# All 72 products of the conditioning row with the ada weights on VectorE

## The chip, the core and the metric

One core of one Trainium2 chip runs the whole layer as one program. The metric is device time in microseconds for one execution; three executions of the kernel before gave 561.93, 562.78 and 564.66 us, and their median, 562.78 us, is the number to beat or to miss. A profiled execution of the same program gives the rows that are shown below.

## What is computed

The reference is one decoder layer on 256 rows of 1024 columns: a half-step SwiGLU FFN (FFN 1), a mixer (attention beside an mLSTM), a second half-step FFN (FFN 2) and a last norm. Each of the three parts is modulated by a shift, a scale and a gate, which come from one row `c`:

```python
mod = (c @ w_ada[l] + b_ada[l]).reshape(B, N_MOD, D_MODEL)      # 9 vectors of 1024
sh1, sc1, g1, sh2, sc2, g2, sh3, sc3, g3 = [mod[:, None, i] for i in range(N_MOD)]
h = modulate(rmsnorm(x, ffn1_norm[l]), sh1, sc1)
x = x + 0.5 * (1 + g1) * swiglu(h, ffn1_w_gate[l], ffn1_w_up[l], ffn1_w_down[l])
h = modulate(rmsnorm(x, mix_norm[l]), sh2, sc2)
x = x + (1 + g2) * hybrid_mixer(h, ...)
h = modulate(rmsnorm(x, ffn2_norm[l]), sh3, sc3)
x = x + 0.5 * (1 + g3) * swiglu(h, ffn2_w_gate[l], ffn2_w_up[l], ffn2_w_down[l])
return rmsnorm(x, final_norm)
```

The product `c @ w_ada` has 9216 columns, which is 72 tiles of 128. These 72 tiles are what the change is about.

## The kernel before

**Layout.** Activations are held transposed: 128 columns on the partitions, 256 rows along the free dimension, eight such tiles `x_sb[:, d]`. Weights are the stationary side of TensorE's products. To keep precision, every weight chunk and every activation is split into a part of 12 bits and its rest, and each product is three matmuls (`mm3`): high by high, low by high, high by low.

**The weight stream.** `chunks` lists the weights in the order of their use, 1 MB each as a rule. `weights()` gives the next one: loads run three chunks ahead, splits one chunk ahead. A split of 1024 columns is two instructions: ScalarE copies the raw weights to `whi` (the 12-bit part), then VectorE subtracts and writes `wlo`. There are four raw buffers, five of `whi` and five of `wlo`; TensorE's products free the split ones.

**The ada tiles.** `ada(col, on_pool)` (L247) loads one tile of 128 x 1024 float32 (512 KB, three buffers named `ada`) and forms the sum of its product with `c_bc`, the row `c` on every partition. It has two ways to do so. With `on_pool` GpSimd multiplies (`prod`, one buffer) and ScalarE sums by copying it with an accumulator (`junk2`, shown as `junk<-prod`). Without, VectorE multiplies and sums in one fused instruction (`junk<-ada,c_bc`), followed by a short read of its accumulator.

**Who calls it.** In FFN 1 `adas(d)` (L402) asks for two tiles for each `d` from 1 on: the shift's one on GpSimd, the scale's one on VectorE; the two of `d` = 0 are asked for in the same way in the start. `fins(d)` then finishes them on VectorE (`fin`, `gs`, `sh`) and makes the modulated norm (`ht`, `hh`, `hl`), which TensorE needs as its moving operand. The other tiles are jobs in a list that `side(...)` (L543) pops at fixed places of FFN 1, the mixer and FFN 2; an argument 1 means GpSimd, 0 VectorE. Of the 72 tiles 43 go to GpSimd and ScalarE and 29 to VectorE; the last eight, during FFN 2, are all on VectorE.

**Order.** The start is written out in order (`ordered(True)`) up to the end of the step `d` = 0 of FFN 1. From there on a scheduler orders each engine's instructions by a simulation of their times, and each engine runs its own list strictly in that order. All loads are issued by the SP queue in program order throughout, so that an ada load that waits for a free buffer holds back the weight loads behind it.

**Stages of the profile.** The start lasts until the first real matmul at 17 us. FFN 1's gate and up products run until about 152 us, its down products until 222 us; then come the mixer, FFN 2, whose last product starts at 547 us, and the last norm. All instructions that go through the ordering helper carry the line L54, so the rows are told apart by tile names.

Of the kernel before, what the change touches and what calls it, by code (L numbers as in the profile page):

```python
# [43 lines left out]
class Ordered:  # L44
    """An engine whose instructions keep the order they are written in while on."""

# [14 lines left out]
def layer(ctx: ExitStack, tc: tile.TileContext, i, out: bass.AP):  # L61
# [39 lines left out]

# [1 line left out]
    c_row = wp.tile([1, D], F32, tag="ada", name="c_row", bufs=3)  # L103
# [6 lines left out]

    # c on every partition, the squares of x; the tensor engine's clock rises with use
    ones_m = const([P, P], F32, "ones_m")
# [47 lines left out]
    for h in range(NH):  # L160
        pool.memset(ohc[:, h, h:h + 1], 1.0)
    # rows h and 32 + h of block h: ones
    oh32 = const([36, NH, P], F32, "oh32")
# [6 lines left out]

# [1 line left out]
    SP = 1024  # L172
# [14 lines left out]
    def load_to(n):  # L187
        """Loads up to chunk n."""
        while len(raws) <= min(n, len(chunks) - 1):
            src = chunks[len(raws)]  # L190
            n1 = src.shape[-1]
            raw = raw_tile()[:, 0:n1]
            cuts = 1 if len(raws) > 3 else 2
            for k in range(cuts):
                sl = slice(k * n1 // cuts, (k + 1) * n1 // cuts)
                dma(raw[:, sl], src[:, sl])
            raws.append(raw)

    def split_piece():
        """Splits the next piece into a part of 12 bits and its rest."""  # L200
        if not parts or len(parts[-1]) * SP >= raws[len(parts) - 1].shape[-1]:
            parts.append([])
        raw, w = raws[len(parts) - 1], parts[-1]
        b = len(w) * SP
        m = min(SP, raw.shape[-1] - b)
        hi = wp.tile([P, SP], F32R, tag="whi", name=nm("whi"), bufs=5)
        lo = wp.tile([P, SP], F32R, tag="wlo", name=nm("wlo"), bufs=5)
        src = raw[:, b:b + m]
        act.activation(hi[:, 0:m], src, AF.Copy)
        dve.tensor_tensor(lo[:, 0:m], src, as32(hi[:, 0:m]), ALU.subtract)  # L210
        w.append((hi, lo))

    def split_to(n):
        """Splits up to chunk n."""
        n = min(n, len(chunks) - 1)
        while len(parts) <= n or len(parts[n]) * SP < raws[n].shape[-1]:
            split_piece()

    def weights(ahead=3):
        """The next chunk, split; loads run ahead by three chunks, splits by one."""  # L220
        n = used[0]
        used[0] += 1
        load_to(n + ahead)
        split_to(n + 1)
        return parts[n]
# [11 lines left out]

# [1 line left out]
    mod = const([P, 72], F32, "mod")  # L239
# [7 lines left out]
    def ada(col, on_pool=False):  # L247
        """mod[:, col] = (c @ w_ada) of the 128 columns from 128 * col."""
        t = wp.tile([P, D], F32, tag="ada", name=nm("ada"), bufs=3)
        dma(t, i["ada"][col])  # L250
        if on_pool:
            pr = wp.tile([P, D], F32, tag="prod", name=nm("prod"), bufs=1)
            pool.tensor_tensor(pr, t, c_bc, ALU.mult)
            junk = wp.tile([P, D], BF16, tag="junk2", name=nm("junk"), bufs=1)
            act.activation(junk, pr, AF.Copy, accum_out=mod[:, col:col + 1])
        else:
            junk = wp.tile([P, D], BF16, tag="junk", name=nm("junk"), bufs=1)
            dve.scalar_tensor_tensor(junk, t, 1.0, c_bc, ALU.mult, ALU.mult,
                                     accum_out=mod[:, col:col + 1])

# [30 lines left out]

# [1 line left out]
    def newton(r0, v, shape, tag, eps=EPS):  # L293
# [5 lines left out]
    def rstd_of(parts, ones=None, tag="m", pre=True, mid=None):  # L299
        """1/sqrt(mean over the partitions of the sum of parts + eps), on every partition."""  # L300
        ps = bank(tag)[:, 0:T]
# [16 lines left out]
    def norm_h(k, d, r, mid=None):  # L318
        """The modulated norm, split."""
        t = t256("ht", bufs=3)  # L320
        dve.scalar_tensor_tensor(t, x_sb[:, d], gs[k][:, d:d + 1], r, ALU.mult, ALU.mult)
        if mid:
            mid()
        act.activation(hh[:, d, 0:T], t, AF.Identity, bias=sh[k][:, d:d + 1])
        dve.scalar_tensor_tensor(hl[:, d, 0:T], t, sh[k][:, d:d + 1], as32(hh[:, d, 0:T]), ALU.add, ALU.subtract)

    def pre_h(k, d):
        """x * gain * (1 + scale), split: the norm before its row factor and shift."""
        act.activation(hh[:, d, 0:T], x_sb[:, d], AF.Copy, scale=gs[k][:, d:d + 1])
# [3 lines left out]
    def pre_shift(k):  # L333
        """The shift, split, as columns T and T + 1."""
        for c in range(2):
# [9 lines left out]
    def add_sq(d, eng):  # L345
        """Squares of x_d into acc; those of the last one stay apart."""
        s = t256("sq", bufs=3)
# [22 lines left out]

# [1 line left out]
    def finish(gh, gl, ft, g, u):  # L372
# [21 lines left out]
    def ffn(k, nxt):  # L394
        nfa = 3
        with tc.tile_pool(name=f"g{k}", bufs=1) as gp:
            gh = gp.tile([P, NF, T], F32R, name=f"gh{k}")
            gl = gp.tile([P, NF, T], F32R, name=f"gl{k}")
            if k == 0:
# [11 lines left out]
                def first(w, ps):  # L411
                    """Columns 0, the parts apart."""
                    for f4 in (0, 4):
# [7 lines left out]
                def outer(w, ps, d, stop, done=None):  # L421
                    """Columns d of 8 tiles of gates and ups."""
                    for ft in range(8):
# [6 lines left out]
                def inner(w, f2, pb, d0, stop):  # L430
                    """Columns d0 to d0 + 3 of one tile of gates and ups."""
                    for d in range(4):
# [110 lines left out]
    def side(*on):  # L543
        """Jobs on the side, on the pool engine (1) or not."""
        for o in on:
            if jobs:
                jobs.pop(0)(o)

# [1 line left out]
    jobs += scale_jobs(1) + gate_jobs(0) + shift_jobs(1) + gate_jobs(1) + scale_jobs(2) + shift_jobs(2)  # L550
    ffn(0, 1)

# [1 line left out]
    # x_m from the norm before its row factor  # L554
    px = [bank("a") for _ in range(4)]
# [11 lines left out]

# [1 line left out]
    with tc.tile_pool(name="fin", bufs=1) as fp:  # L569
# [10 lines left out]
def mixer(tc, nc, i, mp, L):  # L580
# [12 lines left out]
    def tiles(*done):  # L593
        """Two tiles of 128 columns of the input projection, transposed, before row factor and shift."""
        w = weights()
# [7 lines left out]
    def shifted(dst):  # L603
        """Applies row factor and shift."""
        def done(pb):
# [9 lines left out]

# [1 line left out]
    wTv = L["raw_tile"]()  # L617
# [10 lines left out]
    def fold():  # L628
        """Gate weights and query times key weights, taken through the headwise projections."""
        pg = bank("a")  # L630
# [12 lines left out]
        act.activation(wfold[:, 320:832], pqk, AF.Copy, scale=float(P) ** -0.5)  # L643
        # value weights less their mean over the head's channels: the group norm's centring
        vmean = mt([P, NH], "vmean")
# [4 lines left out]

# [1 line left out]
    xm = mt([P, NH, T + 3], "xm", tag="A")  # L652
# [39 lines left out]
    def spread(src):  # L692
        """src's rows, split, for a product that puts one of them on every partition."""
        act.activation(rows[0:4], src, AF.Copy)
# [6 lines left out]
    def gates():  # L701
# [11 lines left out]
        dve.tensor_scalar(gf, pgt[32:36, 0:T], bf, 0.0, ALU.add, ALU.min)  # L713
        # log1p(e) = ln(u) + (e - (u - 1)), u = fl(1 + e)
        lg = mt([NH, T], "lg", tag="R4")
# [12 lines left out]
        spread(nM)  # L728
        # eps * exp(-2 m), kept where its root and the root's square are finite
        em = st["em"] = mt([NH, T], "em", tag="R1")  # L730
# [53 lines left out]
    def m_factors():  # L784
        """The denominators and the group norm's row factor."""
        # 1 / (n sqrt(var / n^2 + eps)) = 1 / sqrt(var + eps n^2), n = max(|den|, exp(-m))
        prow, em = st["prow"], st["em"]
# [10 lines left out]

    # the first tile of the mix on its own: the others take the norm's place after its last use
    mix0 = [mt([P, T], name, F32R) for name in ("mix0h", "mix0l")]  # L800
# [10 lines left out]
    def m_out_pre(h):  # L811
        # (c * norm) * silu(z), (skip * x_conv) * silu(z)
        dve.scalar_tensor_tensor(cn[:, h], cn[:, h], sm[:, C_MN + h:C_MN + h + 1], zs[:, h], ALU.mult, ALU.mult)
        pool.tensor_tensor(xc[:, h], xc[:, h], zs[:, h], ALU.mult)
# [12 lines left out]

# [1 line left out]
    sc = 64 ** -0.5  # L829
# [47 lines left out]
    def turn(j):  # L877
        """Transposes the weights of two heads."""
        for e in range(2):
# [29 lines left out]

# [1 line left out]
    side(1, 0)  # L911
# [96 lines left out]
def _pack(a):  # L1008
    """Layout of the inputs for the kernel: transposes, tiles, zero padding."""
    f = np.float32  # L1010
# [80 lines left out]
```

## Time and profile before

| what | us |
|---|---|
| median of three executions | 562.78 |
| span of the profiled execution (first to last instruction) | 558.7 |
| median less span: what lies around the instructions | 4.1 |
| TensorE (PE) busy, mean granted clock 0.976 | 525.9 |
| VectorE (DVE) busy | 449.8 |
| ScalarE (ACT) busy | 323.9 |
| GpSimd (POOL) busy | 166.9 |

The profiled execution's own time is its span and the 4.1 us around it, which puts it at the median. Busy times of different engines overlap; an engine's idle time costs something only where TensorE waits for it in the end.

### The profile page before, as it was taken

How to read it: one execution, taken by the hardware profiler on the slowest of the kernel's cores; microseconds unless marked ns; L12 is line 12 of the kernel's file. 1: busy time of each engine (PE TensorE's matmuls, PEld its weight loads, DVE VectorE, ACT ScalarE, POOL GpSimd, SP SyncE). 2: the span in 40 equal slices, each digit the busy share in tenths (PEclk: the TensorE clock that was granted, in tenths of full speed). 3: DMA queues.
4: the chain of work that ended last, by engine and by line, in shares of the span. 5: the costliest groups of instructions: out<-in, count | busy, mean ns of one | idle time of the engine just before them, and what ended most of it. 6: DMA issues, size and time to landing. Idle time of an engine off the chain costs nothing.

```text
span 558.7 us, 10327 instructions
## 1 busy us (share of the span) xinstructions
PE 525.9 (94%) x4172; PEld 508.1 (91%) x4172; DVE 449.8 (81%) x626; ACT 323.9 (58%) x572; POOL 166.9 (30%) x107
## 2 busy tenths in 40 slices
PE   7799998999979999699989998999999999999992
PEld 7799998998979999698778888999999999999992
DVE  7989998999889989989987379789987767644423
ACT  5556556676665566567687665676545555544410
POOL 6313413346546766364431002400000000013321
PEclk9799999899989999899999999999999999999997
DMA  8998796367787879865743213478874555545002
GB/s 297 321 363 332 307 351 258 150 225 272 290 307 289 349 284 355 279 261 199 302 187 99 111 59 114 151 264 307 299 249 163 189 189 164 213 157 208 15 0 75
DMA packets 23952, 125.75 MB, mean 225 GB/s; under 512 B 2657, under 2 KB 2913, under 8 KB 14434
## 3 DMA queue, kind: packets, MB, share of 16 engines
q1 hardware_dynamic: 23906, 125.11, 60.8%
q8 instruction: 32, 0.52, 0.4%
q14 instruction: 14, 0.11, 0.1%
HBM read 124.05 MB, written 1.05 MB: 224 GB/s over the span
## 4 chain that ended last, share of the span: by engine, by line
PE 60%; DVE 18%; issue 11%; POOL 5%; ACT 5%; DMA 1%; SPq 0%; DVEq 0%; POOLq 0%; ACTq 0%
PE psa L54 29%; PE psb L54 16%; PE psm L54 14%; DVE wlo L54 8%; POOL prod L54 5%; DVE junk L54 3%; ACT whi L54 2%; ACT junk L54 1%; DVE gm L54 1%; DMA ada<-in_ada 1%; DVE ht L54 1%; DVE mx L54 1%; DVE wfold L54 1%; DVE x L54 1%; DVE hl L54 0%
## 5 line engine op out<-in xcount | busy, mean ns | idle before, releaser
L54 DVE TENSOR_TENSOR wlo<-raw,whi 128x1024 fp32r<-128x1024 f32 (+1 forms) x162 | 229.4, 1423 | 49.2 <-ACT whi L54 48.0
L54 ACT ACTIVATE whi<-raw 128x1024 fp32r<-128x1024 f32 (+1 forms) x162 | 167.6, 1043 | 74.9 <-PE psa L54 39.7
L54 POOL TENSOR_TENSOR prod<-ada,c_bc 128x1024 f32<-128x1024 f32 x43 | 115.2, 2678 | 129.7 <-ACT junk L54 87.0
L54 PE MATMUL psa<-hh,whi 128*128 128x258 f32 (+1 forms) x396 | 110.9, 286 | 4.2 <-DVE x L54 4.0
L54 PE MATMUL psa<-hh,wlo 128*128 128x258 f32 (+1 forms) x396 | 111.2, 286 | 1.3 <-DVE wlo L54 1.3
L54 PE MATMUL psa<-hl,whi 128*128 128x258 f32 (+1 forms) x396 | 110.5, 287 | 0.0
L54 PE MATMUL psb<-hh,whi 128*128 128x258 f32 (+1 forms) x320 | 93.0, 292 | 6.5 <-ACT hh L54 3.9
L54 PE MATMUL psb<-hh,wlo 128*128 128x258 f32 (+1 forms) x320 | 91.7, 288 | 0.0
L54 PE MATMUL psb<-hl,whi 128*128 128x258 f32 (+1 forms) x320 | 90.5, 286 | 0.0
L54 PEld LDWEIGHTS psa<-hh,whi 128*128 128x128 f32 x396 | 75.1, 192 | 4.7 <-DVE x L54 4.2
L54 PEld LDWEIGHTS psa<-hh,wlo 128*128 128x128 f32 x396 | 75.1, 191 | 1.5 <-DVE wlo L54 1.5
L54 PEld LDWEIGHTS psa<-hl,whi 128*128 128x128 f32 x396 | 75.0, 193 | 0.1
L54 PEld LDWEIGHTS psb<-hh,whi 128*128 128x128 f32 x320 | 61.6, 193 | 9.4 <-ACT hh L54 4.1
L54 PEld LDWEIGHTS psb<-hh,wlo 128*128 128x128 f32 x320 | 61.2, 192 | 1.0 <-issue 0.4
L54 PEld LDWEIGHTS psb<-hl,whi 128*128 128x128 f32 x320 | 61.2, 193 | 0.0
L54 POOL TENSOR_SCALAR u_out<-x,sm 128x256 f32<-128x256 f32 x8 | 8.3, 1041 | 166.3 <-DVE x L54 166.3
L54 PE MATMUL psm<-hh,wlo 128*128 128x256 f32 (+1 forms) x204 | 57.6, 285 | 0.1
L54 PE MATMUL psm<-hh,whi 128*128 128x256 f32 (+1 forms) x204 | 57.7, 285 | 0.0
L54 PE MATMUL psm<-hl,whi 128*128 128x256 f32 (+1 forms) x204 | 57.2, 284 | 0.0
L54 PE MATMUL psa<-gh,wlo 128*128 128x256 f32 x176 | 49.5, 282 | 0.0
L54 PE MATMUL psa<-gh,whi 128*128 128x256 f32 x176 | 49.5, 281 | 0.0
L54 PE MATMUL psa<-gl,whi 128*128 128x256 f32 x176 | 49.4, 281 | 0.0
(238 smaller groups left out, 1066.0 us busy)
## 6 DMA issues: line engine op xcount, KB each, us to landing
ada<-in_ada SPq DMA_DIRECT2D x72, 512.0 KB, 5.2
raw<-in_dn SPq DMA_DIRECT2D x22, 1024.0 KB, 5.4
raw<-in_guB SPq DMA_DIRECT2D x19, 1024.0 KB, 4.7
raw<-in_gu SPq DMA_DIRECT2D x18, 1024.0 KB, 7.3
raw<-in_gu SPq DMA_DIRECT2D x8, 512.0 KB, 7.8
raw<-in_wqk SPq DMA_DIRECT2D x4, 1024.0 KB, 7.5
raw<-in_wout SPq DMA_DIRECT2D x4, 1024.0 KB, 4.6
raw<-in_guA SPq DMA_DIRECT2D x4, 768.0 KB, 4.3
```

Source lines behind the costliest of these rows:

```text
L54: r = f(*a, **k)
```

## The change

`ada` loses its branch. The argument `on_pool` stays in the signature and is ignored, so that all callers, and the order of the jobs, stay as they are; every tile takes the fused instruction on VectorE. The buffers `prod` (but for its early use as `zeros`) and `junk2` are no longer used. Elsewhere the diff only takes out comments and docstrings.

```diff
     def ada(col, on_pool=False):
         t = wp.tile([P, D], F32, tag="ada", name=nm("ada"), bufs=3)
         dma(t, i["ada"][col])
-        if on_pool:
-            pr = wp.tile([P, D], F32, tag="prod", name=nm("prod"), bufs=1)
-            pool.tensor_tensor(pr, t, c_bc, ALU.mult)
-            junk = wp.tile([P, D], BF16, tag="junk2", name=nm("junk"), bufs=1)
-            act.activation(junk, pr, AF.Copy, accum_out=mod[:, col:col + 1])
-        else:
-            junk = wp.tile([P, D], BF16, tag="junk", name=nm("junk"), bufs=1)
-            dve.scalar_tensor_tensor(junk, t, 1.0, c_bc, ALU.mult, ALU.mult,
-                                     accum_out=mod[:, col:col + 1])
+        junk = wp.tile([P, D], BF16, tag="junk", name=nm("junk"), bufs=1)
+        dve.scalar_tensor_tensor(junk, t, 1.0, c_bc, ALU.mult, ALU.mult,
+                                 accum_out=mod[:, col:col + 1])
```

## Rows read from the trace of the kernel before

**Rows 1.** Stretches: length, busy us (instructions) by engine, granted clock, DMA share, GB/s

```profile
20.00:80.00 60.00, 59.97 (x490) 59.76 (x490) 57.24 (x75) 34.65 (x46) 19.01 (x7) 0.98 0.89 341
80.00:150.00 70.00, 66.31 (x536) 65.53 (x536) 64.82 (x75) 46.18 (x83) 29.84 (x11) 0.98 0.64 238
150.00:240.00 90.00, 81.94 (x640) 80.32 (x639) 81.90 (x72) 56.66 (x88) 51.98 (x27) 0.94 0.84 312
240.00:300.00 60.00, 57.01 (x433) 50.06 (x432) 56.83 (x106) 43.18 (x102) 23.65 (x12) 1.00 0.59 221
```

**Rows 2.** Waits of PE from 20 to 300 us: total us, times, longest

```profile
PE psa L54 <- DVE x L54: 4.0, 1, 4.0
PE psb L54 <- ACT gh L54: 2.8, 1, 2.8
PE psb L54 <- DVE half L54: 2.1, 1, 2.1
```

**Rows 3.** Instructions on prod, whole span: ns min/median/max, first and last start

```profile
L54 POOL TENSOR_TENSOR prod<-ada,c_bc x43: 2339/2512/4700, 8.7 to 282.5; 128x1024 f32<-128x1024 f32 x43
L54 ACT ACTIVATE junk<-prod x43: 1037/1046/1060, 11.1 to 287.2; 128x1024 bf16<-128x1024 f32 x43
```

**Rows 4.** The same view, 80 to 300 us alone

```profile
L54 POOL TENSOR_TENSOR prod<-ada,c_bc x34: 2369/2516/4700, 87.5 to 282.5; 128x1024 f32<-128x1024 f32 x34
```

**Rows 5.** Timeline at 155 us: start, us, engine, operation

```profile
155.04 2.40 POOL L54 TENSOR_TENSOR prod<-ada,c_bc 128x1024 f32<-128x1024 f32 x1 [1.26 <-ACT junk L54]
155.11 3.41 DVE L54 TENSOR_TENSOR wlo<-raw,whi 128x1024 fp32r<-128x1024 f32 x1
```

**Rows 6.** DVE groups by form, 0 to 300 us: busy us, mean ns, idle before

```profile
L54 DVE TENSOR_TENSOR wlo<-raw,whi 128x1024 fp32r<-128x1024 f32 x85 | 137.0, 1622 | 10.9 <-ACT whi L54 10.8
L54 DVE SCALAR_TENSOR_TENSOR junk<-ada,c_bc 128x1024 bf16<-128x1024 f32 x21 | 37.6, 1789 | 1.1 <-DMA ada<-in_ada 1.1
L54 DVE TENSOR_TENSOR gl<-gm,gh 128x256 fp32r<-128x256 f32 x22 | 18.6, 858 | 1.4 <-ACT gh L54 1.3
...
L54 DVE TENSOR_TENSOR fin<-mod,b 128x1 f32<-128x1 f32 x8 | 7.7, 968 | 0.1
...
L54 DVE TENSOR_TENSOR gm<-sl,half 128x256 f32<-128x256 f32 x8 | 6.5, 807 | 0.1
...
L54 DVE TENSOR_TENSOR sh<-mod,sm 128x1 f32<-128x1 f32 x8 | 3.4, 419 | 0.0
...
L54 DVE TENSOR_TENSOR gs<-fin,sm 128x8 f32<-128x8 f32 x2 | 2.5, 1240 | 0.0
L54 DVE TENSOR_TENSOR gm<-sl,psa 128x256 f32<-128x256 f32 x6 | 2.5, 410 | 0.0
```

**Rows 7.** The same view of DVE, 380 to 560 us

```profile
L54 DVE TENSOR_TENSOR wlo<-raw,whi 128x1024 fp32r<-128x1024 f32 x55 | 67.3, 1223 | 32.3 <-ACT whi L54 31.4
L54 DVE TENSOR_TENSOR gl<-gm,gh 128x256 fp32r<-128x256 f32 x22 | 9.2, 418 | 0.0
L54 DVE SCALAR_TENSOR_TENSOR junk<-ada,c_bc 128x1024 bf16<-128x1024 f32 x7 | 8.5, 1218 | 0.1
```

**Rows 8.** Timeline of the start, 8 to 18 us

```profile
8.63 0.18 DVE L54 TENSOR_SCALAR b<-sm 128x72 f32<-128x72 f32 x1
8.73 2.35 POOL L54 TENSOR_TENSOR prod<-ada,c_bc 128x1024 f32<-128x1024 f32 x1 [1.87 <-DVE ohr L54]
...
9.90 2.27 DVE L54 SCALAR_TENSOR_TENSOR junk<-ada,c_bc 128x1024 bf16<-128x1024 f32 x1 [1.08 <-DMA ada<-in_ada]
...
12.21 0.16 DVE L54 TENSOR_TENSOR fin<-mod,b 128x1 f32<-128x1 f32 x1
...
13.73 2.31 DVE L54 TENSOR_TENSOR sh<-mod,sm 128x1 f32<-128x1 f32 x1
...
17.03 0.80 PE L54 MATMUL psb<-hh,whi 128*128 128x256 f32 x2 [3.89 <-ACT hh L54]
```

**Rows 9.** Waits of POOL, whole span: total us, times, longest

```profile
POOL prod L54 <- DMA ada<-in_ada: 37.5, 5, 16.9
```

## The prediction, made before the changed kernel ran

> **What bounds the kernel now.** I read the busy times first: TensorE has work for 525.9 of 558.7 us, VectorE for 449.8. A mean over the span says little, because GpSimd's products all lie before 290 us, so I cut the span into stretches [rows 1]. The reader should see two things there. From 20 to 80 us TensorE has no gap. From 80 to 300 us it is idle for 3.7 + 8.1 + 3.0 = 14.7 us, and its granted clock is below 1 in two of the three stretches: 0.98 over 70 us and 0.94 over 90 us, which is worth 1.4 + 5.4 = 6.8 us of full-clock work. In all of these stretches VectorE is busy for over nine tenths of the time (57.2 of 60, 64.8 of 70, 81.9 of 90, 56.8 of 60 us), so it is the engine that runs late. The view of waits says the same [rows 2]: the longest waits of TensorE from 20 to 300 us end with VectorE (the residual `x`, `half`), or with ScalarE's `gh`, which itself follows VectorE's `gm`.
>
> Why VectorE is late is seen in the timeline and in its groups. At 155 us GpSimd starts a product of 2.40 us, and 0.07 us later VectorE starts a split that takes 3.41 us [rows 5]. The same split takes 1.223 us on the mean of 55 where no product runs [rows 7]. So VectorE's two-input work stands still while a product of GpSimd is under way. The groups up to 300 us, beside the same operations when undisturbed, give the total [rows 6, 7, 8]:
>
> - `wlo`: 137.0 - 85 x 1.223 = 33.0 us
> - `junk` on VectorE: 37.6 - 21 x 1.218 = 12.0 us
> - `gl`: 18.6 - 22 x 0.418 = 9.4 us
> - `fin`, `sh` and the wide `gs`, at 0.16 us each when undisturbed: 6.4 + 2.1 + 2.2 = 10.7 us
> - `gm<-sl,half`: 6.5 - 8 x 0.41 = 3.2 us (0.41 is the mean of its sister that reads PSUM)
>
> Together 68.3 us, or 1.59 us of VectorE's time for each of the 43 products.
>
> **The change part by part.** It removes 43 products of GpSimd, 2.51 us each, and 43 sums of ScalarE, 1.05 us each [rows 3]. It adds 43 fused instructions to VectorE; the price is that of the seven during FFN 2, where GpSimd multiplies nothing: 1.218 us [rows 7]. That adds 43 x 1.22 = 52.5 us and takes away about 68.3 us of standing still. Each tile moved is thus worth 1.59 - 1.22 = 0.37 us of VectorE's time.
>
> *From 80 to 300 us* lie 34 of the 43 [rows 4]: 34 x 0.37 = 12.6 us less for VectorE, in stretches where TensorE is idle for 14.7 us because of it. I count this in full. The bounds: GpSimd keeps other work (additions into `acc`, masks, the convolution's first tap), so not all of the 68.3 us need be the products'. If a fifth of it stays, a tile is worth 1.27 - 1.22 = 0.05 us, and the term 1.7 us. TensorE can't gain more than its idle 14.7 us.
>
> At this place a rule speaks of more. The Trainium skill (SBUF — State Buffer, Who interferes with whom) says that GpSimd and a VectorE instruction with two SBUF inputs share one read port as an exclusive lock, and that the second to issue waits out the whole instruction of the first. The rows agree in kind: 3.41 - 1.22 = 2.19 us of standing still beside a product of 2.40 us. If every product cost VectorE its full 2.51 us, a moved tile would be worth 1.29 us, VectorE would be relieved by 44 us, and the term would be capped by the 14.7 us; the sum would be 20.1 and the time 542.7 us. The groups show 1.59 us, since a product can also fall where VectorE reads PSUM or is itself first; I stay with the rows.
>
> *The clock.* After a long gap TensorE runs on at the lower of its two levels for a while; the stretch with the waits of 4.0 and 2.8 us is the one with 0.94 [rows 1, 2]. Those two gaps should shrink, not all vanish. I take half of the 6.8 us, 3.4, with bounds 0 and 6.8.
>
> *The start* runs in the written order. VectorE's first fused instruction took 2.27 us and the tiny `sh` 2.31 us, beside products of GpSimd [rows 8]. Undisturbed they cost 1.22 and 0.16 us, so 1.05 + 2.15 = 3.2 us go. The added fused instruction for the shift's first tile fits between the end of `b` at 8.81 us and the landing that starts the next one at 9.90; it ends at 10.03 and costs 0.13. So the first real matmul, now at 17.03 us, could come 3.0 us earlier. From 20 to 80 us the DMA share is 0.89 with TensorE never idle, and the loads behind the start move up less: the second weight chunk waits for an ada buffer that the first product frees at about 11.1 us and that is now free at 10.0. So 1.0 to 3.0 us; I take 2.0.
>
> *From 20 to 80 us* VectorE is relieved too, by 7 tiles' worth, but TensorE has no gap to close there: nothing. The cover is the load stream, and if it tears, see the second rival.
>
> *ScalarE* loses 45 us of sums and *GpSimd* about 108 us. Neither ends a wait of TensorE by its own load: nothing, beyond that `whi` and `gh` come a little sooner. *The SP queue*: an ada buffer is now freed by VectorE's instruction. Weight loads stand behind ada loads, but no split waits for a raw weight now (VectorE's `wlo` waits for `whi` alone, 10.8 us in 300 [rows 6]). I take nothing. *FFN 2* has all its eight tiles on VectorE already: nothing. After 300 us nothing changes.
>
> Sum: 12.6 + 3.4 + 2.0 = 18.0 us. Against the span of 558.7 that is 540.7; with the 4.1 us around it, 544.8 us, where the profiled execution and the median stand at 562.8. The bounds give 562.8 - (1.7 + 0 + 1.0) = 560.1 and 562.8 - (14.7 + 6.8 + 3.0) = 538.3.
>
> **The rivals.** *The gaps are of the order, not of the load.* TensorE's gaps stand at the ends of stages (the last `gh` before the down products, the last residual before the mixer). If they are the length of a chain and VectorE's place in its list, rather than its backlog, they stay, and only the lower bounds come: 559 to 560 us. For it: the two longest waits are single events at such ends. Against it: the chains through them run over splits and fused instructions that took 3.41 instead of 1.22 us.
>
> *VectorE stands before a load* (slower). GpSimd waited 37.5 us in five waits for ada tiles, 16.9 in the longest [rows 9], with only the next product behind it. On VectorE, which keeps its list's order, all splits, residuals and norms stand behind such an instruction, and TensorE waits for the splits. If the scheduler's idea of the landing is as early as it was for GpSimd, and all of it reaches TensorE, the price is 37.5 us against the gain of 18.0: about 582 us. It decides once more than 18 us of such waits come through. Against it: the 21 fused instructions that VectorE already runs up to 300 us wait for the same stream, and lost 1.1 us to it [rows 6].
>
> *The standing still is not the products' doing.* Then VectorE simply gets 41 x 1.22 = 50.0 us more from 20 to 300 us, where it has 260.8 of 280 busy: 310.8, which is 30.8 us too many, and the time is 562.8 + 30.8, about 594 us. Against it: the undisturbed 1.223 us over 55 splits, in a stretch without products. The Trainium skill has a rule on this side (Perfetto Trace Analysis, Optimizing Scalar/DVE Operations): if VectorE is saturated, handing some of its work to ScalarE or even GpSimd may make sense. The page adds that between VectorE and GpSimd it might not help, because of the port, as in [rows 5].
>
> **How the numbers follow.** The forecast's own range is 538 to 552 us, chance 0.62. A gain beyond it, below 538: 0.04 (the clock at the start may come up sooner too). The first rival, or a mixture of it with the forecast, 552 to 562 us: 0.20, of which 0.12 is faster than by 0.5% (below 560.0) and 0.08 within it. The second rival: 0.08 slower, and 0.02 where it just eats the gain. The third: 0.04. That makes 0.78 faster, 0.10 the same within 0.5%, which is about what a measurement of this kernel can tell from no change, and 0.12 slower. The range is 535 to 562 us: it takes in both ends of the bounds and the first rival, and leaves out the slower cases and a part of the unchanged ones.
>
> **What would show it.** Right: splits and `gl` up to 300 us at 1.22 and 0.42 us but for those beside GpSimd's `acc`; VectorE's busy time down by some 16 us although it has 43 instructions more; the first real matmul at 14 to 16 us; the waits for `x` and `gh` at the ends of FFN 1's parts shorter; the clock from 150 to 240 us nearer 1; nothing changed after 300 us but the offset. Wrong: fused instructions idle before ada loads, with the splits behind them late (second rival); gaps of the same length at the same places while VectorE has idle time (first); splits still at 1.6 us on the mean (third).

## The result, and the profile after

The changed kernel takes 547.66 us (median of four executions, 544.78 to 550.38) against 563.6 for the kernel before, measured beside it; the ratio is 0.9716 with a 95% interval of 0.9672 to 0.9759. The forecast was 544.8 us, with its own range from 538 to 552. The profiled execution has a span of 543.0 us, 15.7 less than before.

First the page of the changed kernel: busy time of each engine.

```profile
PE 520.8 (96%) x4172; PEld 502.2 (92%) x4172; DVE 419.6 (77%) x712; ACT 281.6 (52%) x486; POOL 48.8 (9%) x64
```

VectorE has 86 instructions more (43 fused ones and their reads of the accumulator) and is busy for 30.2 us less (449.8 before). The groups of VectorE up to 300 us show where that comes from; they answer to [rows 6] (busy us, mean ns, idle before).

```profile
L54 DVE TENSOR_TENSOR wlo<-raw,whi 128x1024 fp32r<-128x1024 f32 x89 | 108.7, 1227 | 15.4 <-ACT whi L54 15.3
L54 DVE SCALAR_TENSOR_TENSOR junk<-ada,c_bc 128x1024 bf16<-128x1024 f32 x64 | 77.9, 1218 | 8.0 <-DMA ada<-in_ada 7.8
L54 DVE TENSOR_TENSOR gl<-gm,gh 128x256 fp32r<-128x256 f32 x22 | 8.7, 417 | 0.0
...
L54 DVE SCALAR_TENSOR_TENSOR gm<-xm,sm,gm 128x256 f32<-128x256 f32 x12 | 5.6, 477 | 0.3 <-POOL gm L54 0.3
...
L54 DVE TENSOR_TENSOR gm<-sl,half 128x256 f32<-128x256 f32 x8 | 3.3, 416 | 0.0
```

The split fell from 1.622 to 1.227 us, `gl` from 0.858 to 0.417, `gm<-sl,half` from 0.807 to 0.416: the first two are now at the price they had before in stretches without products [rows 7], the last at that of its sister that reads PSUM [rows 6].

The stretches answer to [rows 1], with the start and the time after 300 us beside them (length, busy us of PE, PEld, DVE, ACT, POOL, granted clock, DMA share, GB/s).

```profile
0.00:20.00 20.00, 16.77 (x112) 15.76 (x112) 17.08 (x35) 8.36 (x12) 5.96 (x20) 1.00 0.86 319
20.00:80.00 60.00, 56.50 (x464) 55.87 (x465) 52.46 (x86) 29.22 (x35) 0.00 (x0) 1.00 0.90 351
80.00:150.00 70.00, 68.27 (x569) 67.87 (x568) 65.53 (x110) 39.52 (x68) 0.00 (x0) 1.00 0.83 311
150.00:240.00 90.00, 90.00 (x753) 88.52 (x751) 77.60 (x123) 46.53 (x72) 10.57 (x13) 1.00 0.81 297
240.00:300.00 60.00, 60.00 (x418) 49.25 (x418) 45.62 (x109) 39.01 (x103) 2.48 (x3) 1.00 0.48 175
300.00:380.00 80.00, 76.30 (x592) 72.69 (x591) 62.05 (x110) 48.32 (x93) 11.70 (x12) 0.98 0.48 171
```

The same two stretches of the kernel before, which [rows 1] does not have:

```profile
0.00:20.00 20.00, 13.96 (x78) 13.13 (x79) 16.19 (x25) 9.96 (x14) 10.65 (x22) 0.90 0.86 303
300.00:380.00 80.00, 77.99 (x602) 71.43 (x602) 58.25 (x108) 54.05 (x118) 13.64 (x13) 1.00 0.39 138
```

From 80 to 300 us TensorE is now idle for 1.7 us where it was for 14.7, and its granted clock is 1.00 where it was 0.94 to 1.00. But two stretches are worse than before: it is idle for 3.5 us from 20 to 80 us, where it had no gap, and for 3.7 us from 300 to 380 us (2.0 before).

The start answers to [rows 8]; the last three rows are TensorE's products that begin the first, the second and the third weight chunk.

```profile
8.78 1.21 DVE L54 SCALAR_TENSOR_TENSOR junk<-ada,c_bc 128x1024 bf16<-128x1024 f32 x1
...
10.03 1.23 DVE L54 SCALAR_TENSOR_TENSOR junk<-ada,c_bc 128x1024 bf16<-128x1024 f32 x1
...
12.83 0.15 DVE L54 TENSOR_TENSOR sh<-mod,sm 128x1 f32<-128x1 f32 x1
...
14.02 0.50 PE L54 MATMUL psb<-hh,whi 128*128 128x256 f32 x2 [0.84 <-ACT hh L54]
...
21.04 0.39 PE L54 MATMUL psb<-hh,whi 128*128 128x256 f32 x1 [1.09 <-ACT whi L54]
...
30.11 0.39 PE L54 MATMUL psb<-hh,whi 128*128 128x256 f32 x1 [1.02 <-ACT hh L54]
```

Before, the second and the third chunk began like this:

```profile
25.38 0.28 PE L54 MATMUL psb<-hh,whi 128*128 128x256 f32 x1
...
31.17 0.28 PE L54 MATMUL psb<-hh,whi 128*128 128x256 f32 x1
```

The first product comes 3.0 us earlier (17.03 before), as the working had it. The first chunk then gains more: its products keep TensorE busy for 5.9 us at a granted clock of 1.00, where they took 8.35 us at 0.65, so that they end 5.4 us earlier. But then TensorE waits four times, 1.09 and 0.20 us for `whi`, 1.24 for `wlo` and 1.02 for `hh`. These 3.5 us are all its gaps from 20 to 80 us. The second chunk's products, broken up by these waits, also keep TensorE busy for 6.6 us in place of 5.8. So the third chunk begins at 30.11 us in place of 31.17: 1.1 us are left of the 5.4.

TensorE's waits from 300 to 380 us show the other loss, a gap at the first output product that did not exist before:

```profile
PE psm L54 <- ACT mix0h L54: 2.3, 1, 2.3
PE psm L54 <- DVE mix0l L54: 1.4, 1, 1.4
```

With these marks the 15.7 us split up. The first output product (reading `mix0h`) started at 330.8 us before and at 313.9 after. From the third chunk to there the kernel took 330.8 - 31.2 = 299.6 us and takes 313.9 - 30.1 = 283.8: 15.8 less. The start adds 1.1. From there to the end it took 227.9 and takes 229.1: 1.2 lost. The wait of 2.3 us for `mix0h` lies ahead of that mark, inside the 15.8; behind it TensorE is idle for 11.4 us in place of 12.0 and busy for 217.7 in place of 215.9, with a granted clock of 0.72 in the 6 us behind the mark, where it was 1.00 before.

### The profile page after: what moved, and what is told of

Same layout as the page of the kernel before. It is cut to its first block, busy times and chain, and to the rows that moved or that the text cites. A ratio compares the mean times of both kernels' runs of the same rounds, so it can differ in the third digit from the quotient of the medians.

```text
span 543.0 us, 10281 instructions
## 1 busy us (share of the span) xinstructions
PE 520.8 (96%) x4172; PEld 502.2 (92%) x4172; DVE 419.6 (77%) x712; ACT 281.6 (52%) x486; POOL 48.8 (9%) x64
## 4 chain that ended last, share of the span: by engine, by line
PE 90%; DVE 5%; DMA 2%; ACT 1%; issue 1%; SPq 0%; DVEq 0%; ACTq 0%
PE psa L54 42%; PE psb L54 26%; PE psm L54 22%; DVE junk L54 2%; DMA raw<-in_gu 1%; DMA x<-in_x 1%; DVE wlo L54 1%; DVE u_out L54 0%; ACT whi L54 0%; DVE nw L54 0%; DVE oa L54 0%; ACT sq L54 0%; SPq L97 0%; DVEq L1080 0%; DVE rr L54 0%
## 5 line engine op out<-in xcount | busy, mean ns | idle before, releaser
L54 DVE TENSOR_TENSOR wlo<-raw,whi 128x1024 fp32r<-128x1024 f32 (+1 forms) x162 | 196.2, 1215 | 53.3 <-ACT whi L54 52.2
L54 PE MATMUL psa<-hl,whi 128*128 128x258 f32 (+1 forms) x396 | 109.4, 283 | 0.0
L54 DVE SCALAR_TENSOR_TENSOR junk<-ada,c_bc 128x1024 bf16<-128x1024 f32 x72 | 87.7, 1218 | 8.9 <-DMA ada<-in_ada 8.7
L54 PE MATMUL psb<-hh,wlo 128*128 128x258 f32 (+1 forms) x320 | 90.5, 284 | 1.2 <-DVE wlo L54 1.2
L54 PEld LDWEIGHTS psb<-hh,whi 128*128 128x128 f32 x320 | 60.4, 189 | 6.8 <-ACT whi L54 3.0
L54 PEld LDWEIGHTS psm<-hh,whi 128*128 128x128 f32 x204 | 38.5, 189 | 0.1
```

Of the source, the lines that this page charges most:

```text
L54: r = f(*a, **k)
```

## The experiments

Each kernel below was timed beside the kernel before on the same chip; ratios are to that one, with 95% intervals.

**Is it GpSimd's reading, the order, or ScalarE?** The scheduler places the instructions anew after any edit, and the change also took 45 us of sums off ScalarE, so the end of VectorE's standing still had two rivals. In the first kernel GpSimd gets idle products back:

```diff
         dve.scalar_tensor_tensor(junk, t, 1.0, c_bc, ALU.mult, ALU.mult,
                                  accum_out=mod[:, col:col + 1])
+        if on_pool:
+            pool.tensor_tensor(t, c_bc, c_bc, ALU.mult)
```

> The changed kernel, with 43 idle products added on GpSimd: after each moved tile's fused instruction, GpSimd multiplies c_bc by itself into the tile's buffer, which nobody reads. No result of GpSimd is waited for except by the buffer's next load. If what the change took away was VectorE standing still beside GpSimd's products, about 1.6 us for each comes back on a VectorE that now also carries the 52 us of fused instructions: VectorE's busy time up by some 68 us over the changed kernel's 419.6, splits up to 300 us at about 1.6 us on the mean again, and a time of 575 to 600 us, worse than both kernels. If the gain came from the new order of the instructions, or from work taken off ScalarE, the time stays at 545 to 551 us and the splits at 1.23 us.

Measured: 584.94 us, ratio 1.037 (1.033 to 1.041). VectorE's busy time is 483.7 us, 64.1 more than in the changed kernel, for the same instructions. In the groups up to 300 us:

```profile
L54 DVE TENSOR_TENSOR wlo<-raw,whi 128x1024 fp32r<-128x1024 f32 x82 | 123.7, 1513 | 3.7 <-ACT whi L54 3.7
...
L54 DVE TENSOR_TENSOR gm<-sl,half 128x256 f32<-128x256 f32 x8 | 11.2, 1400 | 0.0
```

Products whose results nobody uses cost 37 us. The second kernel keeps GpSimd busy in the same places without reading:

```diff
+        if on_pool:
+            for _ in range(3):
+                pool.memset(t, 0.0)
```

> The changed kernel, with GpSimd filling the tile's buffer with zeros three times after each moved tile's fused instruction: GpSimd is busy in the same places, holds the ada buffer as the first experiment does, but reads nothing. If VectorE stands still only beside GpSimd's reading of SBUF, splits stay at 1.23 us and the time at 546 to 553 us. If it stands still beside any work of GpSimd in SBUF, splits are slow here too, in proportion to GpSimd's busy time, and the time goes to 560 us and above. If the later freeing of the ada buffer were what costs in the first experiment, this one is slowed as much.

Measured: 549.88 us, ratio 0.9753 (0.9718 to 0.9789), within the spread of the changed kernel. VectorE's split takes 1.221 us on the mean up to 300 us; the second row is the stretch from 80 to 150 us, where GpSimd is busy for 45.42 us:

```profile
L54 DVE TENSOR_TENSOR wlo<-raw,whi 128x1024 fp32r<-128x1024 f32 x88 | 107.3, 1221 | 22.7 <-ACT whi L54 22.4
```

```profile
80.00:150.00 70.00, 68.27 (x557) 67.86 (x556) 65.08 (x109) 37.80 (x62) 45.42 (x48) 0.98 0.79 303
```

So it is GpSimd's products that stop VectorE's split, not any work of GpSimd in SBUF, and not the ada buffer being held for longer, which both kernels do (the SP queue waits 70.7 us for GpSimd's products and 54.9 us for its zeros up to 300 us). A product and a filling differ in arithmetic as well as in reading, and no run here separates the two. That the reading is what counts is what the Trainium skill states (SBUF — State Buffer, Who interferes with whom): a VectorE instruction with two SBUF inputs contends with a GpSimd instruction that reads SBUF and not with one that only writes. The two runs agree with it.

One more rival lies in the loads: in the kernel before, the SP queue waited 128.2 us up to 300 us for products to free ada buffers, with weight loads behind. The trace of before speaks against it: from 20 to 300 us ScalarE's copies to `whi` waited only 0.5 us for raw weights.

The third kernel puts the sums back on ScalarE:

```diff
+    spare = const([P, 72], F32, "spare")
...
+        if on_pool:
+            j2 = wp.tile([P, D], BF16, tag="junk2", name=nm("junk"), bufs=1)
+            act.activation(j2, t, AF.Copy, accum_out=spare[:, col:col + 1])
```

> The changed kernel, with the 43 sums put back on ScalarE as idle work: ScalarE copies the ada tile and sums it into a spare column, 1.05 us each with a read of the accumulator. If the relief of ScalarE had a part in the gain, the time goes up by several us, to 551 to 556. If it had none, 546 to 551 us, and what moves is the order of the instructions alone.

Measured: 547.39 us, ratio 0.9715 (0.9684 to 0.9746), with ScalarE busy for 326.0 us as before the change. Its relief had no part that shows beyond the spread. VectorE's list here differs from the changed kernel's at many places too, so here a new order moved little.

**What do the added instructions cost?**

```diff
+        if on_pool:
+            dve.tensor_copy(mod[:, col:col + 1], t[:, 0:1])
+            return
```

> The changed kernel without the 43 moved products: the tiles are loaded, and VectorE copies one column of each instead of multiplying (the shift, gate and scale values are then other numbers). VectorE has some 46 us less to do. This prices the added instructions on the path. If VectorE still sets the pace up to 300 us after the change, the time falls by 5 us or more, below 543. If TensorE and the load stream now set it, 544 to 548 us: the added 52 us are then nearly free, and all that the change brought is the end of the standing still.

Measured: 534.0 us, ratio 0.9487 (0.9451 to 0.9523). The added fused instructions are not nearly free: they cost 547.7 - 534.0 = 13.7 us on the path by the medians, and 543.0 - 532.1 = 10.9 by the spans of the two profiled executions, of which that of the changed kernel is the fastest of its four. The gain of the change is thus a difference: the end of the standing still and of the products is worth some 29 us (563.4 - 534.0), and the fused instructions take 11 to 14 of it back. The profile says where. TensorE has no gap of more than 0.2 us from 20 to 300 us:

```profile
20.00:80.00 60.00, 59.80 (x499) 59.59 (x499) 47.15 (x79) 30.25 (x35) 0.00 (x0) 1.00 0.87 345
80.00:150.00 70.00, 70.00 (x589) 70.00 (x588) 53.50 (x102) 40.72 (x71) 0.00 (x0) 1.00 0.92 344
150.00:240.00 90.00, 90.00 (x739) 87.69 (x738) 66.20 (x113) 45.53 (x74) 12.08 (x13) 1.00 0.82 300
240.00:300.00 60.00, 60.00 (x429) 49.18 (x429) 38.71 (x100) 40.64 (x108) 3.49 (x3) 1.00 0.36 132
```

Its third chunk begins at 26.1 us, not 30.1, with the same loads. So 4.0 us are lost in the start. The first output product starts at 302.8 us, not 313.9, so 7.1 us more are lost between these two marks: 1.7 in a gap at about 100 us (waits of 1.15 and 0.58 us), 2.3 in the wait ahead of the output product, and 3.1 by which TensorE is busy for longer at the same clock of 1.00. Where these last lie is open.

**Do the two halves add?** One kernel moves only the eight first tiles of FFN 1, one only the 35 jobs:

```diff
-                    ada(d, d > 0)
+                    ada(d)
...
-                             mid=lambda: (warm(16), ada(0, True), ada(8), load_to(0), scale_fin(0, 0, 1)))
+                             mid=lambda: (warm(16), ada(0), ada(8), load_to(0), scale_fin(0, 0, 1)))
```

> The kernel before with only the eight first tiles of FFN 1 that GpSimd had moved to VectorE; the 35 jobs stay on GpSimd and ScalarE. By the prediction's steps only the start term comes: first matmul at 14.0 us, 1 to 3 us in all, 560 to 562 us, and the gaps at the ends of FFN 1's parts stay. If the gain is made by new places in the order and not by the tiles moved, it may come out anywhere from 550 to 565.

Measured: 560.64 us, ratio 0.9945 (0.9917 to 0.9973): 3 us, and TensorE still idle for 8.0 us from 150 to 240 us. Its first product comes at 14.07 us, but its third chunk at 30.98, 0.2 us earlier than before the change.

```diff
-        if on_pool:
+        if on_pool and col < 8:
```

> The kernel before with only the 35 jobs moved to VectorE; the eight first tiles stay on GpSimd. By the prediction's steps this takes the 12.6 and 3.4 us and leaves the start: 546 to 549 us, first matmul at 17.0 us, splits at 1.6 us or slower before 80 us and at 1.22 after. If the eight first tiles make the room for the rest, it gains less than 8 us.

Measured: 547.23 us, ratio 0.9714 (0.9675 to 0.9753): 16.4 us, all of the gain, with the first product at 17.2 us. The splits before 80 us took 1.302 us on the mean and not 1.6 as expected (1.398 before the change), those after 80 us 1.237. By the medians the halves don't add: 3.0 + 16.4 would be 19.4, both together give 15.9. But the difference of 3.5 us is within what the intervals leave open. What the traces show is that the first tiles' gain at the first product is given back by the third chunk whether the jobs are on GpSimd (30.98 us) or on VectorE (30.11).

**Where the start is given back.** Three theories: ada loads that wait for a buffer and hold back the weights, the rate of the loads, or VectorE's list. A fourth ada buffer:

> The changed kernel with four ada buffers in place of three. After the change TensorE reaches its third weight chunk at 30.1 us, though it starts 3.0 us earlier; without the moved products it reaches it at 26.1. If the weight loads of the start are held back by ada loads that wait for a buffer which VectorE now frees later, a fourth buffer lets them go: third chunk at 27 to 28 us, time 544 to 546. If the start is held by VectorE's own list (two fused instructions ahead of the norm of the next step) or by the rate of the loads, nothing moves: 547 to 548.

Measured: 545.58 us, ratio 0.9683 (0.9654 to 0.9711), with the third chunk at 30.1 us as before it. The weights of the third chunk were issued earlier (11.6 us on, with SP no longer waiting for an ada buffer there) and reached ScalarE at 22.4 us, as in the other kernels. So the buffer theory fell; whether the 2 us between the medians are real is open, as the intervals overlap. Next, ScalarE's copies of the second chunk written ahead of step 1's norm, VectorE's subtractions behind it:

> The changed kernel with one thing moved in the start: for step 0 ScalarE's two copies of the second weight chunk are written ahead of the norm of step 1, and VectorE's two subtractions behind it, so that they come ahead of the second of step 2's fused instructions. In the changed kernel these subtractions start at 22.7 us, behind a fused instruction that waits for its load; without the moved products they start at 19.7. If VectorE's own list is what gives back the start (a fourth ada buffer left the third chunk at 30.1 us), the third chunk comes at 27 to 29 us and the time falls by 1 to 3 us, to 544.5 to 546.5. If the rate of the loads gives it back, the third chunk stays at 30 us and the time at 547 to 548.

Measured: 548.73 us, ratio 0.9733 (0.9706 to 0.9759). The theory as I put it failed: neither of the two outcomes came. The subtractions started only at 22.14 us in place of 22.70, since the scheduler's next fused instruction waits 1.14 us for its load in front of them, and the third chunk began at 32.2 us, later than before, behind a wait of 2.25 us for `hh`:

```profile
20.59 1.23 DVE L54 SCALAR_TENSOR_TENSOR junk<-ada,c_bc 128x1024 bf16<-128x1024 f32 x1 [1.14 <-DMA ada<-in_ada]
...
22.14 2.35 DVE L54 TENSOR_TENSOR wlo<-raw,whi 128x1024 fp32r<-128x1024 f32 x2
```

What stands is that the moved products lose the 4.0 us (without them the third chunk is at 26.1 us although its weights land no earlier); which of VectorE's and ScalarE's places in the list does it is not settled.

**A better place for the jobs.** If VectorE's load costs at 100 us and in the mixer, the jobs should go where it has room:

```diff
-                    side(1, 1)
+                    side(1)
...
-    QF, QD, jobs = ((1,), (), (0,)), (((1,), (1, 0)), ((), ()), ((), ())), []
+    QF, QD, jobs = ((1, 1), (), (0,)), (((1, 1), (1, 1)), ((), ()), ((), ())), []
```

> The changed kernel with the jobs at other places: one in place of two at each of the four inner steps of FFN 1, two in place of one at its six last gate and up steps, two at each step of its down products; so four or so are left to the mixer in place of twelve. Without the moved products the gap at 100 us (2.4 us) and 4.7 us of the mixer are gone, so VectorE's load there is what they cost. If the fused instructions can be moved to where VectorE has room, the time falls by 3 to 6 us, to 542 to 545. If VectorE has no room in the down products either, it stays or rises: 546 to 550.

Measured: 540.35 us, ratio 0.9582 (0.9547 to 0.9618), more than expected. (The 2.4 us of the expectation is the sum of three waits for `whi`, two of them in the start; the gap at about 100 us is 1.7.) VectorE's stretches are the mirror of the changed kernel's: 85.91 in place of 77.60 us from 150 to 240, 38.17 in place of 45.62 from 240 to 300, and TensorE is not slowed in either:

```profile
150.00:240.00 90.00, 90.00 (x753) 88.95 (x753) 85.91 (x142) 47.77 (x79) 11.65 (x13) 1.00 0.86 331
240.00:300.00 60.00, 60.00 (x438) 50.11 (x435) 38.17 (x92) 43.36 (x109) 3.36 (x4) 1.00 0.35 130
```

The gap ahead of the output product is gone as well: the first one starts at 309.8 us, although the third chunk begins only at 32.4. With the moved splits on top, and then with four ada buffers too:

> The jobs at the other places of the fourth experiment of the second set (540.4 us) and the moved splits of the start together. If the two act in different places, their gains add: 537 to 540 us. If the start is bound by the loads, 540 to 541.

Measured: 541.53 us, ratio 0.9605 (0.9582 to 0.9628): the moved splits bring nothing here either.

> Both of these and four ada buffers: the best version that the runs point to. The fourth buffer alone gave 545.6 against 547.7 us, with the third chunk where it was, so its part may be chance of the order; 536 to 540 us if the three add, 538 to 541 if the buffer brings nothing.

Measured: 539.15 us, ratio 0.9562 (0.9539 to 0.9586), the lowest time of a kernel that computes the whole layer. What it has over the moved jobs alone, 540.35 us, lies within the intervals.

## Why the prediction was right, point by point

- **The cause.** VectorE stands still beside GpSimd's reading products: shown by the idle products (37 us slower) and the zeros (549.88 us, within the spread). The third rival, that the standing still was not the products' doing, is out.
- **The term from 80 to 300 us and the clock, 12.6 + 3.4 = 16.0 us.** From the third chunk to the output product 15.8 us came, and the kernel with the jobs alone gained 16.4. That the sum fits so well is in part luck. Between these marks TensorE's idle time fell from 14.8 to 4.0 us, by 10.8 and not 12.6, and its busy time from 284.8 to 279.8, by 5.0 and not 3.4: the clock rose from 0.98 to 1.00, so it came back in full in these stretches (1.00 in all three), not by half. VectorE's relief was mis-sized too: its busy time fell by 30.2 us in all, 0.70 us for each tile and not 0.37, because groups left out of the working stood still as well (`gm<-xm` fell from 8.0 to 5.6 us, the two forms of `hl` together by 3.2). And it does not count in full: between the marks VectorE has 29.9 us less to do, and 10.8 of that reached TensorE's idle time. Twice the relief, a third of it counted, came near half the relief counted in full.
- **"VectorE's two-input work stands still."** Right for the groups of the working, but too narrow: `wfold`, which reads one raw tile and a column, took 0.851 us on the mean of four before and 0.333 after.
- **The start, 2.0 us between 1.0 and 3.0.** The upper bound came at the first product (3.0), the lower one at the third chunk (1.1). The sum had no term for the clock of the first chunk, which gave 2.4 us more (8.35 to 5.9 us), nor for the waits behind it, which took more than that away. The reason given for the lower bound, the load stream behind a buffer, is not the cause: a fourth buffer changed nothing there. The moved products are, since the third chunk comes at 26.1 us without them; by which engine's list is open.
- **"From 20 to 80 us: nothing."** Wrong: 3.5 us of gaps appeared, which had no cover. All of them lie up to the start of the third chunk, so they are the same loss as in the start, not a second one. The second rival, VectorE before a load, did come, at 7.8 us of waiting up to 300 us instead of 37.5, and not enough to decide.
- **"After 300 us nothing changes."** Wrong by 2.3 us ahead of the output product and by 1.2 behind it. The latter is the clock's, and it need not follow from that wait: in the kernel with the jobs at other places, which does not have it, the time from the output product to the end is 229.1 us as well.
- **The first rival**, gaps that belong to the order and not to the load, failed for the gaps at the ends of FFN 1's parts: both closed without an edit to the chain, and TensorE's idle time from 150 to 240 us stayed at 8.0 us where the jobs were left on GpSimd and the list was ordered anew.
- **The offset of 4.1 us.** It was the median less the span of another execution. The changed kernel's profiled execution took 544.78 us with a span of 543.0, so only 1.8 us lie around the instructions and the rest is the spread between executions. In the 35 later executions of the kernel before, the time is 1.8 to 3.1 us more than the span, and no span is below 558.8: its profile, with 558.7, is of a fast execution and does not stand at the median. That of the changed kernel is the fastest of four as well (clock 0.992, the others 0.981 to 0.987). So the two profiles can be compared, and the difference of the medians, 15.9 us, and that of the spans, 15.7, agree.
- **The sum.** Of 18.0 us 15.7 came in the spans: 0.9 less in the start, 0.2 less up to the output product, and 1.2 lost after it.

## What to carry to other kernels

An engine that takes work over can slow down the one it relieves. Here each product of 2.5 us on GpSimd, made to spare VectorE a fused instruction of 1.22 us, cost VectorE more than those 1.22 us in standing still (1.59 by the working's groups), and it is read off by comparing one operation's mean in a stretch with and without the helper. Then price the instruction that comes back as well, by leaving it out: it may cost on the path, and moving it to a stretch with room on that engine (7 us here) can bring half as much again as the change.

## What the runs showed of the hardware that I had not expected

GpSimd's filling with zeros, 45.42 us busy in a stretch of 70, left VectorE's two-input split at 1.221 us. And the granted clock in the first 20 us went from 0.90 to 1.00: the wait of TensorE between the products that keep it busy at the start and its first real one shrank from 3.89 to 0.84 us, so that it ran on at the higher of its two levels, 2.4 and 1.2 GHz (the first chunk at 1.00 in place of 0.65), and was 5.4 us ahead by the end of the first chunk, not only 3.0. With a wait of 4.06 us there, in the kernel with the jobs alone, the first chunk's clock was 0.82; with 2.41, in the one with idle products, 1.00.
